# A hybrid attention layer on one core: the feed-forward part's instructions kept in the written order, a scale per token half, a pipelined output projection and spread sums

## The chip, the core and the metric

The kernel runs on one core of one Trainium2 chip. The metric is the device time of one execution in microseconds. The engines are called as in the profile: PE (TensorE, matrix products; PEld is its load of weights), DVE (VectorE), ACT (ScalarE), POOL (GpSimd) and SP (SyncE, whose queue issues the transfers). Each engine takes its instructions strictly in the order of its queue.

## What is computed

One layer over 2048 tokens of 1024 features: modulated RMS norm, an input projection, forgetting attention and differential attention, an output projection, and a modulated SwiGLU feed-forward part with 2816 hidden features. The change touches the last two steps, and a norm in the first.

```python
h = _modulate(x, ln1_g[l], sh1, sc1)
u = h @ w_in[l]
...
mixed = jnp.concatenate([fox_out, diff_out], axis=-1)
x = x + g1[:, None, :] * (mixed @ w_out[l])

h2 = _modulate(x, ln2_g[l], sh2, sc2)
y = (jax.nn.silu(h2 @ w_gate[l]) * (h2 @ w_up[l])) @ w_down[l]
x = x + g2[:, None, :] * y
```

## The kernel before

**Numbers in two halves.** PE multiplies 16-bit numbers. A 32-bit operand is scaled by a power of two and split into a high and a low half: `cast_scaled` (L139, on ACT) writes the high half, `sub_scaled` (L144, on DVE) the difference. Three products of halves make one product. The power of two comes from the operand's largest magnitude: `absmax` (L123) takes it per partition on DVE, `colmax` (L108, L109) spreads it over the partitions by a small PE matmul against an identity and reduces the result, `pow2` (L115 to L119) makes scale and inverse. So each scale is a chain DVE, PE, DVE, and PE stands at L108 until DVE has the maximum.

**Stages.** 0 to 150 us: first norm and modulation, with `first_norm` for each of the 16 blocks of 128 tokens. 150 to 1350: eight head groups of projection and attention, as streams merged by `run`. Then `out_proj` (L934) for the 16 blocks: it loads a tile of `mixed`, splits it, turns it round with a transposing transfer (L928, issued by SP), runs two halves of 24 matmuls, adds the result to x (L936), stores it as `x1d`, and takes the row's root mean square (L940 on ACT, `rsqrt`). Blocks 0 to 9 run merged with the last attention group, blocks 10 to 15 afterwards.

**Feed-forward.** 22 pairs `q`: 11 pairs of weight tiles for each of two halves of the tokens. A pair has 14 slots. Slot by slot, for `w` = gate and then up, one of seven `product`s (L1091, 12 matmuls of 512 columns each, a seven-product scheme over 2x2 blocks, in the order of `ORDER`). Its results leave PSUM through `s4s` (L1094), `s5s` (L1096), `dif` (L1101) on ACT and sums on DVE and POOL (L1097 is POOL's s4s - s5s). Beside them stand the 16 `down`s of the pair before (L1149, six matmuls each, added to x by L1153), spread over the slots by `DOWNAT`. What prepares operands is put into a slot by `at`:

- gate and up weights: `gu_load`, `gu_bound` (the maximum, 128x2048), `gu_sum` (L1038, five sums on POOL), `gu_scale` (with L108), `gu_split` in three parts (1024, 1536, 1024 wide);
- down weights: `dn_load` (transfer, maximum L1061, product L1062 on POOL), `dn_scale` (with L108), `dn_split`;
- the activation of the pair before: `act_scale` (maximum of the whole 128x2048 tile, L108) and `act_split` for each token half.

The normalised rows' sums for the seven products (`norm_row` L974 and L975, `norm_sum` L984 to L989) are made for blocks 0 to 7 next to the projection, and for blocks 8 to 15 in pairs 2, 4, 6 and 8: two rows are loaded again, normalised, and seven sums follow at slots 10 to 13. They go to `hcd` in memory and come back when the token halves change (pair 10).

**What sets the order.** The kernel is written for Tile, whose scheduler simulates the engines and places instructions as it expects them to become ready; the written order gives the dependences and the priorities. So in the kernel before neither a slot nor a stream fixes where an instruction stands on its engine. `bufs` is the number of buffers behind a name: a small tile can be written again only when its readers are done.

Of the kernel before, what the change touches and what calls it, by code (L numbers as in the profile page):

```python
# [55 lines left out]
def trunk(ctx, tc, t):
# [860 lines left out]
    def out_proj(blk):  # L917
        if blk == 0:
            hs.extend(htile() for _ in range(4))
        x1 = pairbuf(blk // 2)[:, blk % 2, :]  # L920
        rows = slice(blk * P, (blk + 1) * P)
        nc.sync.dma_start(x1, t["x"][rows, :])
# [382 lines left out]
```

## Time and profile before

| | us |
|---|---|
| median of three runs | 2928.06 |
| lowest, highest | 2925.38, 2935.83 |
| the profiled execution | 2939.51 |
| its span | 2937.7 |
| PE busy in it | 2728.9 (93%) |
| DVE busy | 2111.3 (72%) |
| POOL busy | 1609.5 (55%) |
| ACT busy | 1441.2 (49%) |
| mean granted clock of PE | 0.98 |

The profiled execution is 11.45 us above the median; all times of rows are its own, in microseconds from the start of its span. A PE group that runs without a gap shows the time of its matmuls one behind the other; idle time ahead of a group stands in brackets with what ended it. A wait is listed under the line that waited and the line that released it. The clock is the share of full speed that PE was granted; 1.00 is 2.4 GHz and 0.5 is 1.2 GHz. Shares over the whole span mix stages with different limits, so the stretches are read one by one.

### The profile page before, as it was taken

What the parts mean: (1) busy time and instruction counts of PE and PEld (TensorE: products, weight loads), DVE (VectorE), ACT (ScalarE), POOL (GpSimd) and SP (SyncE); (2) the same over time, 40 slices, a digit from 0 to 9 for tenths busy, and PEclk for the clock granted to TensorE, in tenths of its full rate; (3) what the DMA queues carried; (4) which work ended last, traced back from release to release, by engine and by line L of the source; (5) the groups of instructions that cost most, each with busy time, mean ns of one, the idle gap of its engine ahead of it and who ended that gap; (6) DMA issues with size and microseconds to landing.
All of it is one profiled execution on the core that took longest, in us unless ns stands there. A gap on an engine that the chain in (4) does not pass through costs nothing.

```text
span 2937.7 us, 49384 instructions
## 1 busy us (share of the span) xinstructions
PE 2728.9 (93%) x18902; PEld 1479.9 (50%) x18902; DVE 2111.3 (72%) x4077; ACT 1441.2 (49%) x2725; POOL 1609.5 (55%) x1392
## 2 busy tenths in 40 slices
PE   5789989899999999999989998899999999999998
PEld 3456656566665655664444343444444444444443
DVE  7786675857758686656744887787878778778775
ACT  4666667666676777786543422333323332233230
POOL 2566666665667787675542645444545444535430
PEclk9899999999999999999999999999999999999999
DMA  6232231322224233234776223224234511112101
GB/s 230 77 82 61 63 73 39 82 53 67 73 50 94 53 105 95 49 103 118 171 196 202 85 68 98 72 79 110 70 108 150 165 59 57 58 52 64 58 22 58
DMA packets 269902, 261.92 MB, mean 89 GB/s; under 512 B 204376, under 2 KB 221144, under 8 KB 263904
## 3 DMA queue, kind: packets, MB, share of 16 engines
q1 hardware_dynamic: 269664, 258.75, 31.0%
q8 instruction: 148, 2.42, 0.4%
q14 instruction: 90, 0.74, 0.1%
HBM read 173.55 MB, written 36.91 MB: 72 GB/s over the span
## 4 chain that ended last, share of the span: by engine, by line
PE 52%; DVE 21%; DMA 12%; POOL 6%; ACT 6%; issue 4%; SPq 0%; POOLq 0%; DVEq 0%; ACTq 0%
PE ps_mx L1149 10%; PE ps_ip L437 10%; PE ps_st L1091 7%; PE ps_pv L1091 6%; DMA stg<-in_w_ada_dram 3%; PE ps_ip L934 3%; DMA stg<-stg 2%; PE ps_mx L1091 2%; PE ps_st L579 2%; DVE t_mxc L548 2%; PE ps_st L580 2%; PE ps_pv L609 2%; PE ps_mx L546 2%; PE ps_pv L608 2%; PE ps_pv L607 2%
## 5 line engine op out<-in xcount | busy, mean ns | idle before, releaser
L593 POOL TENSOR_TENSOR pxs<-pxs 128x512 f16<-128x512 f32 (+3 forms) x640 | 683.3, 1082 | 325.8 <-ACT pxs L590 191.8
L1091 PEld LDWEIGHTS <-mt 128*128 128x128 f16 x3696 | 361.8, 99 | 446.7 <-issue 22.0
L437 PE MATMUL ps_ip<-wbuf,ht 128*128 128x384 f16 (+1 forms) x2952 | 560.6, 332 | 26.1 <-DVE vts L144 13.5
L1149 PE MATMUL ps_mx<-wide,ht 128*128 128x512 f16 x2112 | 505.4, 382 | 11.5 <-ACT ht L139 5.6
L1038 POOL TENSOR_TENSOR pxm<-vts 128x512 f32<-128x512 f32 x220 | 295.7, 1370 | 347.1 <-DMA vts<-in_w_gu_dram 316.3
L585 ACT ACTIVATE pxs<-ps_st,cells 128x512 f32<-128x512 f32 (+3 forms) x640 | 388.7, 619 | 142.5 <-PE ps_st L580 68.9
L437 PEld LDWEIGHTS <-ht 128*128 128x128 f16 x3072 | 295.7, 99 | 243.5 <-issue 46.2
L1091 PE MATMUL ps_st<-ht,mt 128*128 128x512 f16 x1584 | 383.0, 386 | 5.6 <-ACT mt L1094 3.2
L1091 PE MATMUL ps_pv<-ht,mt 128*128 128x512 f16 x1584 | 383.3, 380 | 1.1 <-ACT mt L1096 1.1
L590 ACT ACTIVATE pxs<-pxs 128x512 f16<-128x512 f32 (+3 forms) x640 | 350.7, 565 | 16.4 <-PE ps_pv L609 7.6
L607 PE MATMUL ps_pv<-vts,pxs 128*128 128x129 f16 (+1 forms) x2176 | 342.6, 207 | 4.2 <-DVE os L626 3.1
L608 PE MATMUL ps_pv<-vts,pxs 128*128 128x128 f16 (+1 forms) x2176 | 344.7, 208 | 0.0
L1149 PEld LDWEIGHTS <-ht 128*128 128x128 f16 x2112 | 206.3, 98 | 266.7 <-issue 16.9
L609 PE MATMUL ps_pv<-vts,pxs 128*128 128x129 f16 (+1 forms) x2176 | 325.6, 207 | 9.8 <-POOL pxs L593 8.9
L548 DVE TENSOR_REDUCE t_mxc<-ps_mx 128x1 f32<-128x512 f32 x384 | 256.9, 682 | 93.8 <-PE ps_mx L546 92.0
L1153 DVE SCALAR_TENSOR_TENSOR mt<-ps_mx,t_ai,mt 128x512 f32<-128x512 f32 x352 | 256.6, 743 | 75.5 <-PE ps_mx L1149 75.2
L607 PEld LDWEIGHTS <-pxs 128*128 128x128 f16 x2176 | 208.2, 97 | 56.7 <-ACT pxs L585 3.5
L579 PE MATMUL ps_st<-mt 67*128 67x512 f16 (+7 forms) x640 | 223.8, 350 | 10.4 <-ACT pxs L585 10.2
L609 PEld LDWEIGHTS <-pxs 128*128 128x128 f16 x2176 | 206.8, 99 | 50.0 <-POOL pxs L593 24.3
L608 PEld LDWEIGHTS <-pxs 128*128 128x128 f16 x2176 | 208.0, 97 | 35.3 <-issue 4.1
L580 PE MATMUL ps_st<-mt 128*128 128x512 f16 (+3 forms) x640 | 223.8, 350 | 0.0
L546 PE MATMUL ps_mx<-mt 71*128 71x512 f16 (+7 forms) x640 | 197.3, 350 | 19.6 <-DVE t_mxc L548 13.1
(266 smaller groups left out, 4097.0 us busy)
## 6 DMA issues: line engine op xcount, KB each, us to landing
vts<-in_w_gu_dram SPq DMA_DIRECT2D x44, 1024.0 KB
stg<-in_w_down_dram SPq DMA_DIRECT2D x44, 512.0 KB
stg<-in_w_ada_dram SPq DMA_DIRECT2D x32, 512.0 KB
stg<-in_w_in_dram SPq DMA_DIRECT2D x24, 512.0 KB
mt<-in_w_ada_dram SPq DMA_DIRECT2D x16, 512.0 KB
mt<-mt SPq DMA_DIRECT2D x128, 64.0 KB
mixed<-os SPq DMA_DIRECT2D x32, 256.0 KB
stg<-in_w_out_dram SPq DMA_DIRECT2D x16, 512.0 KB
```

The source lines that it names most:

```text
L437: T.matmul(pt[:, 0:N], lhsT=h4[:, k, hs, c : c + P], rhs=w4[k // 4][:, k % 4, ws, 0:N], start=(i == 0), stop=(i == len(terms) - 1))
L548: V.tensor_reduce(out=mx[:, 4 * j + n : 4 * j + n + 1], in_=b[:, 0:w], op=ALU.max, axis=AX.X)
L579: T.matmul(b[:, c0:QC], lhsT=K2[0:K, kb * P : (kb + 1) * P], rhs=QA[0:K, q0:q1], start=True, stop=False, skip_group_check=True)
L585: A.activation(p32[:, c0:QC], b[:, c0:QC], AF.Exp, bias=pshift, scale=1.0)
L590: A.activation(ph[:, c0:QC], p32[:, c0:QC], AF.Copy, bias=0.0, scale=1.0)
L593: (V if hilo[1] == "V" else G).tensor_tensor(out=pl[:, c0:QC], in0=p32[:, c0:QC], in1=ph[:, c0:QC], op=ALU.subtract)
L607: T.matmul(pv[:, jj, :], lhsT=lhs_h, rhs=v4[:, kb, h, 0 : W + 1], start=first, stop=False, skip_group_check=True)
L608: T.matmul(pv[:, jj, 0:W], lhsT=lhs_h, rhs=v4[:, kb, h, W + 2 : 2 * W + 2], start=False, stop=False, skip_group_check=True)
L609: T.matmul(pv[:, jj, :], lhsT=lhs_l, rhs=v4[:, kb, h, 0 : W + 1], start=False, stop=end, skip_group_check=True)
L1038: G.tensor_tensor(out=sums[:, k * 512 : (k + 1) * 512], in0=raw[:, a * 512 : (a + 1) * 512], in1=raw[:, b * 512 : (b + 1) * 512], op=op)
L1091: T.matmul(b.rearrange("p (b n) -> p b n", b=4), lhsT=aw[w][:, APOS[i] * 4 + k, ws, :], rhs=cb[:, :, 2 * k + hb, :], start=(fresh and k == ...
L1149: T.matmul(b, lhsT=aT[:, th, as_, f, j * P : (j + 1) * P], rhs=dnb[:, (2 * q + f) % 4, ws, n * 512 : (n + 1) * 512], start=(f == 0 and z = ...
```

## The change

- `Ordered` wraps an engine: each instruction issued through it is kept in program order. From the feed-forward part on (and for the functions called after that line, `out_proj` 10 to 15 among them) V, A, G and T, that is DVE, ACT, POOL and PE, are wrapped. SP isn't.
- The activation's scale is taken per token half: `act_bound` reduces 128x1024, `act_scale` makes scale and inverse, `act_split` follows. The first half's stand in slots 11, 12, 13 of the pair itself, the second half's in slots 0, 1, 2 of the next.
- `ORDER` and `DOWNAT` change; `dn_load` moves to slots 1 and 2 and its maximum becomes `dn_bound` at 3 and 4; `dn_split` moves from slots 9 and 10 to 6 and 7. The sum `tmp + dif` moves to product 3.
- Blocks 8 to 15 of the normalised rows: `late_row` inside the output projection writes them to `yd`; `late_sum` cuts each of the 28 sums into load, add (two slots on), low half (three), transpose (four) and store (five), three sums per pair, beginning at slots 6, 9 and 13. In a slot the late steps stand ahead of the others.
- `out_load` and `out_split` of the next block stand inside the current one, the split between its two halves.
- The head of the feed-forward part is put between the blocks 10 to 15.
- First norm: `first_stats` makes the row scales of four blocks together for token chunks 1 to 3. The small maxima have four buffers instead of two.

```diff
+class Ordered:
...
+        def issue(*args, **kw):
+            ins = f(*args, **kw)
+            if hasattr(ins, "ins"):
+                self.tc.keep_in_program_order(ins)
+            return ins
...
-        am = small(1, "am" if dt == F32 else "amh", bufs=2, dt=dt)
-        V.tensor_reduce(out=am, in_=src, op=ALU.max, axis=AX.X, apply_absolute_value=True)
+        am = small(1, "am" if dt == F32 else "amh", bufs=4, dt=dt)
+        V.tensor_reduce(out=am, in_=src, op=ALU.max, axis=axis, apply_absolute_value=True)
...
-            rows.append((1, lambda j=j: first_norm(j)))
+            rows.append((0.5, lambda j=j: first_scale(j, r4)))
...
+        if blk + 1 < NB:
+            out_load(blk + 1)
...
+            if n == 0 and blk + 1 < NB:
+                out_split(blk + 1)
...
+        if blk > 8:
+            late_row(blk - 1)
...
-    ORDER = (4, 5, 1, 2, 3, 7, 6)
+    ORDER = (4, 5, 1, 2, 7, 3, 6)
...
+    def late_row(blk):
+
+        y = pairbuf(blk // 2)[:, blk % 2, :]
+        norm_rows2(y, blk)
+        nc.sync.dma_start(yd[blk - 8], y)
...
+        def add():
+            e = st["e"]
+            if other:
+                G.tensor_tensor(out=e[:, 0:512], in0=e[:, 0:512], in1=e[:, 512:1024], op=op)
+            s3, hi, _, _ = parts()
+            A.activation(hi, s3, AF.Copy, bias=0.0, scale=1.0)
...
+        return [(0, load), (2, add), (3, low), (4, turn), (5, store)]
...
+    V, A, G, T = Ordered(tc, V), Ordered(tc, A), Ordered(tc, G), Ordered(tc, T)
...
+    def act_bound(q, th):
+        sets[q]["aam", th] = absmax(act[:, th], BF16, axis=AX.XY)
...
     gu_load(0, 0)
+    run(outs[10:11])
     gu_bound(0, 0)
     for k in range(5):
         gu_sum(k)
+    run(outs[11:13])
     gu_scale(0, 0)
+    run(outs[13:14])
     for k in range(3):
         gu_split(0, 0, k)
-    run(outs[10:16])
+    run(outs[14:16])
+    late_row(15)
...
-    DOWNAT = (0, 0, 0, 0, 2, 2, 2, 2, 2, 2, 1, 1, 1, 1)
+    DOWNAT = (0, 1, 1, 1, 1, 1, 2, 1, 1, 2, 2, 2, 1, 0)
...
+    for k, steps in enumerate([late_sum(jj, i) for jj in range(4, 8) for i in ORDER]):
+        for d, f in steps:
+            late[14 * (k // 3) + (6, 9, 13)[k % 3] + d].append(f)
...
-                at(3 + f, dn_load, q, f)
+                at(1 + f, dn_load, q, f)
+                at(3 + f, dn_bound, q, f)
             at(5, dn_scale, q)
             for f in range(2):
-                at(9 + f, dn_split, q, f)
+                at(6 + f, dn_split, q, f)
+        if q < NQP:
+            at(11, act_bound, q, 0)
+            at(12, act_scale, q, 0)
+            at(13, act_split, q, 0)
         if q:
-            at(0, act_scale, q - 1)
-            at(1, act_split, q - 1, 0)
+            at(0, act_bound, q - 1, 1)
+            at(1, act_scale, q - 1, 1)
             at(2, act_split, q - 1, 1)
...
-                for _ in range(DOWNAT[slot]):
+                for _ in range(DOWNAT[slot] if q < NQP else (3, 2, 2, 1, 8)[slot] if slot < 5 else 0):
...
-            for f in st[slot]:
+            for f in late[14 * q + slot] + st[slot]:
```

In the instruction streams of the changed kernel every wrapped instruction has the line L65, that of the wrapper. Three places show what moves.

DVE at the end of the output projection (`ht<-ps_ip` and `ht<-ps_mx` add a projection's half to x, `t_rq` and `cells` are the row scale, `t_amh<-vts` is `gu_bound`), before:

```order
L134 TENSOR_TENSOR t_rq_22005<-t_rq_22005,t_nv 128x1
L135 SCALAR_TENSOR_TENSOR cells<-t_rq_22005,t_ry_22003 128x1
L936 SCALAR_TENSOR_TENSOR ht<-ps_ip,cells,ht 128x512
L936 SCALAR_TENSOR_TENSOR ht<-ps_mx,cells,ht 128x512
L942 TENSOR_SCALAR t_nv<-t_nss 128x1
L1099 TENSOR_TENSOR pxm<-ps_st,mt 128x512
L133 SCALAR_TENSOR_TENSOR t_rq_22076<-t_ry_22074 128x1
L109 TENSOR_REDUCE t_cm<-ps_ip 128x1
L134 TENSOR_TENSOR t_rq_22076<-t_rq_22076,t_nv 128x1
L115 TENSOR_SCALAR t_p2a<-t_cm 128x1
L135 SCALAR_TENSOR_TENSOR cells<-t_rq_22076,t_ry_22074 128x1
```

and after:

```order
L65 SCALAR_TENSOR_TENSOR ht<-ps_ip,cells,ht 128x512
L65 SCALAR_TENSOR_TENSOR ht<-ps_mx,cells,ht 128x512
L65 TENSOR_SCALAR t_nv<-t_nss 128x1
L65 SCALAR_TENSOR_TENSOR t_rq_21984<-t_ry_21982 128x1
L65 TENSOR_TENSOR t_rq_21984<-t_rq_21984,t_nv 128x1
L65 SCALAR_TENSOR_TENSOR cells<-t_rq_21984,t_ry_21982 128x1
L65 SCALAR_TENSOR_TENSOR ht<-ht,cells,vts 128x1024
L65 TENSOR_TENSOR ht<-ht,vts 128x1024
L65 SCALAR_TENSOR_TENSOR ht<-ht,cells,vts 128x1024
L65 TENSOR_TENSOR ht<-ht,vts 128x1024
L65 TENSOR_REDUCE cells<-grep_21994 128x1
L65 TENSOR_REDUCE t_amh<-vts 128x1
```

Before, the products' sums (`pxm<-ps_st`) come in between, and the maximum of the second weight tile stands further ahead. After, the row scale of the last block, the late rows of blocks 14 and 15 (four passes over 128x1024) and the maximum of `grep2` stand ahead of `t_amh<-vts`.

DVE in slots 3 to 5 of a middle pair (`mt<-ps_mx,t_ai` is a down's L1153, `t_dam<-stg` the maximum of a down weight, `t_amh<-vts` `gu_bound`, `t_cm<-ps_ip` the step behind L108, `t_amh<-t_dam` the maximum for `dn_scale`), before, from the activation's maximum on:

```order
L1153 SCALAR_TENSOR_TENSOR mt<-ps_mx,t_ai,mt 128x512 x4
L1120 TENSOR_TENSOR pxm<-ps_mx,pxm 128x512
L144 SCALAR_TENSOR_TENSOR mt<-pxm,t_ws,mt 128x8x128
L1153 SCALAR_TENSOR_TENSOR mt<-ps_mx,t_ai,mt 128x512
L123 TENSOR_REDUCE t_amh<-uhm 128x1
L123 TENSOR_REDUCE t_amh<-vts 128x1
L1099 TENSOR_TENSOR pxm<-ps_st,mt 128x512
L109 TENSOR_REDUCE t_cm<-ps_ip 128x1
L123 TENSOR_REDUCE t_amh<-t_dam 128x1
L115 TENSOR_SCALAR t_p2a<-t_cm 128x1
```

and after:

```order
L65 SCALAR_TENSOR_TENSOR mt<-ps_mx,t_ai,mt 128x512
L65 TENSOR_REDUCE t_dam<-stg 128x1
L65 TENSOR_REDUCE t_amh<-vts 128x1
L65 TENSOR_TENSOR mt<-ps_pv,pxm 128x512
L65 SCALAR_TENSOR_TENSOR mt<-ps_mx,t_ai,mt 128x512
L65 TENSOR_REDUCE t_dam<-stg 128x1
L65 TENSOR_REDUCE t_cm<-ps_ip 128x1
```

for slots 3 and 4, and for slot 5, from the last step of `gu_scale` on:

```order
L65 TENSOR_SCALAR t_gi<-t_gi,cells 128x1
L65 TENSOR_TENSOR wide<-ps_pv,wide 128x512
L65 SCALAR_TENSOR_TENSOR mt<-ps_mx,t_ai,mt 128x512
L65 TENSOR_REDUCE t_amh<-t_dam 128x1
L65 TENSOR_REDUCE t_cm<-ps_ip 128x1
```

Before, one maximum of the activation and one of the weight follow each other, and the one for `dn_scale` stands behind several other steps. After, the maxima stand directly behind a down's evacuation, the last of them (`t_amh<-t_dam`) with nothing else in between.

ACT at the start of a pair with a late sum (`mt<-ps_st` is `s4s`, `mt<-ps_pv` `s5s`, `mt<-vts,t_ws` and `mt<-pxm,t_ws` the three casts of `gu_split`, `stg<-stg` the cast of a normalised rows' sum, `ht<-uhm` the activation's cast), before:

```order
L1094 ACTIVATE mt<-ps_st 128x512
L988 ACTIVATE stg<-stg 128x4x128
L1096 ACTIVATE mt<-ps_pv 128x512
L139 ACTIVATE mt<-pxm,t_ws 128x8x128
L988 ACTIVATE stg<-stg 128x4x128
L1101 ACTIVATE wide<-ps_st 128x512
L988 ACTIVATE stg<-stg 128x4x128
L1094 ACTIVATE mt<-ps_st 128x512
L139 ACTIVATE ht<-uhm,t_as 128x1024 x2
L139 ACTIVATE mt<-vts,t_ws 128x8x128
L139 ACTIVATE mt<-pxm,t_ws 128x12x128
L1103 ACTIVATE uhm<-ps_st,t_gi 128x512
```

and after:

```order
L65 ACTIVATE mt<-ps_st 128x512
L65 ACTIVATE mt<-vts,t_ws 128x8x128
L65 ACTIVATE mt<-ps_pv 128x512
L65 ACTIVATE stg<-stg 128x4x128
L65 ACTIVATE mt<-pxm,t_ws 128x12x128
L65 ACTIVATE mt<-pxm,t_ws 128x8x128
L65 ACTIVATE ht<-uhm,t_as 128x1024
L65 ACTIVATE wide<-ps_st 128x512
```

Before, the sums' casts come four near one another, between the evacuations. After, there is one in this stretch, directly behind `s5s` and ahead of the second and third cast of the weight.

## Rows read from the trace of the kernel before

**Rows 1.** Busy time by stretch: columns us, then busy us of each engine, clock, DMA share, GB/s

```profile
1532.00:1603.00 71.00, 62.79 (x285) 27.92 (x283) 31.06 (x49) 16.18 (x28) 20.38 (x13) 0.95 0.69 214
...
1603.00:2342.00 739.00, 688.71 (x3135) 306.65 (x3132) 578.78 (x827) 236.37 (x279) 375.93 (x241) 0.97 0.33 102
...
2342.00:2900.00 558.00, 557.94 (x2606) 253.54 (x2607) 426.70 (x634) 169.78 (x191) 236.56 (x161) 1.00 0.15 50
```

**Rows 2.** PE's waits, 1603 to 2938: waiting line, releaser, us in all, times, longest

```profile
PE ps_ip L108 <- DVE t_amh L123: 36.9, 8, 7.3
```

**Rows 3.** PE's waits, 150 to 1603

```profile
PE ps_ip L934 <- DMA wide<-wide: 5.7, 3, 2.3
```

**Rows 4.** Timeline of PE, five stretches: start, us, line, count, [idle before <-releaser]

```profile
1413.41 7.04 PE L934 MATMUL ps_ip<-mt,wide 128*128 128x512 f16 x24 [2.27 <-DMA wide<-wide]
...
1569.24 5.78 PE L934 MATMUL ps_mx<-mt,wide 128*128 128x512 f16 x26
...
1975.83 1.47 PE L1149 MATMUL ps_mx<-wide,ht 128*128 128x512 f16 x6 [1.14 <-ACT ht L139]
...
2211.52 4.44 PE L1149 MATMUL ps_mx<-wide,ht 128*128 128x512 f16 x12 [2.06 <-DVE mt L1153]
...
2902.64 1.46 PE L1149 MATMUL ps_mx<-wide,ht 128*128 128x512 f16 x6
...
2908.59 0.29 PE L108 MATMUL ps_ip<-idb,t_amh 128*128 128x128 bf16 x1 [4.50 <-DVE t_amh L123]
...
2910.88 23.08 PE L1149 MATMUL ps_mx<-wide,ht 128*128 128x512 f16 x96 [2.00 <-ACT ht L139]
```

**Rows 5.** Timeline of DVE at the end, 2902 to 2910

```profile
2902.84 0.69 DVE L1120 TENSOR_TENSOR pxm<-ps_mx,pxm 128x512 f32<-128x512 f32 x1 [1.84 <-PE ps_mx L1091]
...
2904.14 0.75 DVE L1153 SCALAR_TENSOR_TENSOR mt<-ps_mx,t_ai,mt 128x512 f32<-128x512 f32 x1 [0.61 <-PE ps_mx L1149]
...
2906.25 2.29 DVE L123 TENSOR_REDUCE t_amh<-uhm 128x1 bf16<-128x2048 f32 x1 [1.36 <-POOL uhm L1126]
...
2908.92 0.29 DVE L109 TENSOR_REDUCE t_cm<-ps_ip 128x1 f32<-128x128 f32 x1 [0.39 <-PE ps_ip L108]
...
2909.43 0.15 DVE L116 TENSOR_SCALAR t_as<-t_p2a 128x1 int32<-128x1 int32 x1
...
2909.51 0.14 DVE L118 TENSOR_SCALAR t_p2b<-t_p2a 128x1 f32<-128x1 f32 x1
...
2909.87 0.27 DVE L1136 TENSOR_SCALAR t_ai<-t_ai,t_di,t_gi 128x1 f32<-128x1 f32 x1
```

**Rows 6.** DVE by shape, 1603 to 2938: shapes xcount, busy us, mean ns, idle before

```profile
L144 DVE SCALAR_TENSOR_TENSOR mt<-pxm,t_ws,mt 128x1536 f16<-128x1536 f32 x43 | 81.6, 1897 | 1.8 <-ACT mt L139 1.8
...
L144 DVE SCALAR_TENSOR_TENSOR mt<-pxm,t_ws,mt 128x1024 f16<-128x1024 f32 x43 | 72.5, 1687 | 6.3 <-ACT mt L139 5.6 <-POOL mt L1097 0.7
...
L144 DVE SCALAR_TENSOR_TENSOR mt<-vts,t_ws,mt 128x1024 f16<-128x1024 f32 x43 | 59.4, 1381 | 5.1 <-ACT mt L139 4.2
...
L144 DVE SCALAR_TENSOR_TENSOR ht<-uhm,t_as,ht 128x1024 f16<-128x1024 f32 x44 | 55.7, 1296 | 9.3 <-ACT ht L139 9.2
...
L1061 DVE TENSOR_REDUCE t_dam<-stg 128x1 f32<-128x1024 f32 x41 | 49.3, 1210 | 13.4 <-DMA stg<-in_w_down_dram 12.9
```

**Rows 7.** ACT by shape, 1603 to 2938

```profile
L139 ACT ACTIVATE mt<-pxm,t_ws 128x1536 f16<-128x1536 f32 x43 | 67.2, 1563 | 26.4 <-DVE t_ws L116 26.4
...
L139 ACT ACTIVATE mt<-vts,t_ws 128x1024 f16<-128x1024 f32 x43 | 49.0, 1141 | 106.7 <-PE ps_mx L1149 59.1 <-DVE t_p2b L118 35.5 <-DVE t_gi L119 10.4
...
L1094 ACT ACTIVATE mt<-ps_st 128x512 f32<-128x512 f32 x43 | 25.3, 589 | 66.1 <-PE ps_st L1091 66.1
```

**Rows 8.** POOL by shape, 1603 to 2938

```profile
L1097 POOL TENSOR_TENSOR mt<-mt 128x512 f32<-128x512 f32 x44 | 62.7, 1424 | 60.3 <-ACT mt L1096 60.3
...
L984 POOL TENSOR_TENSOR stg<-stg 128x512 f32<-128x512 f32 x20 | 29.5, 1473 | 103.3 <-DMA hcd<-stg 101.0 <-DVE wide L144 2.4
```

**Rows 9.** Timeline of SP's queue, one transpose

```profile
1409.65 1.33 SPq L928 DMA_TRANSPOSE wide<-wide  x1
```

More of the change, by code (lines that the diff above doesn't have):

```diff
@@ L292, in first_norm, with first_stats, first_scale @@
         norm_rows(xt, xt)
+    def first_stats(c, r4):
+        ss = small(4, "dss", bufs=2)
+        for j in range(4):
+            A.activation(sqs.bitcast(F16), xcs[c][:, j, :], AF.Square, bias=0.0, scale=1.0, accum_out=ss[:, j : j + 1])
+        V.tensor_scalar(out=ss, in0=ss, scalar1=1.0 / D, scalar2=EPS, op0=ALU.mult, op1=ALU.add)
+        r = small(4, "drr", bufs=2)
+        rsqrt(ss, r, 4)
+        r4["r"] = r
+    def first_scale(blk, r4):
+        xt = xcs[blk // 4][:, blk % 4, :]
+        G.tensor_scalar(out=xt, in0=xt, scalar1=r4["r"][:, blk % 4 : blk % 4 + 1], scalar2=0.0, op0=ALU.mult, op1=ALU.add)
     def first_hT(blk):
@@ L915, in pairbuf, with out_load, out_split @@
         return t.rearrange("p (b n) -> p b n", b=2)
[L917 to L922, printed above, removed]
+    oin = {}
+    def out_load(blk):
         mt = stage()
-        nc.sync.dma_start(mt, mixed[rows, :])
+        nc.sync.dma_start(mt, mixed[blk * P : (blk + 1) * P, :])
+        oin[blk] = mt
+    def out_split(blk):
+        mt = oin.pop(blk)
         mh, mT = scr[:, 0], scr[:, 1 + blk % 2].rearrange("p s (k n) -> p s k n", k=KT)
@@ L928, in out_proj @@
         nc.sync.dma_start(mT.rearrange("p s k n -> p (s k) n"), mh.rearrange("p s n -> p (s n)"), transpose=True)
+    def out_proj(blk):
+        if blk == 0:
+            hs.extend(htile() for _ in range(4))
+            out_load(0)
+            out_split(0)
+        mT = scr[:, 1 + blk % 2].rearrange("p s (k n) -> p s k n", k=KT)
+        x1 = pairbuf(blk // 2)[:, blk % 2, :]
+        rows = slice(blk * P, (blk + 1) * P)
+        nc.sync.dma_start(x1, t["x"][rows, :])
+        if blk + 1 < NB:
+            out_load(blk + 1)
         for n in range(2):
@@ L1107, in product @@
             V.tensor_tensor(out=dif, in0=b, in1=dif, op=ALU.subtract)
+            G.tensor_tensor(out=tmp, in0=tmp, in1=dif, op=ALU.add)
             if w == 0:
@@ L1112, in product @@
         elif i == 7:
+            V.tensor_tensor(out=s5s, in0=b, in1=tmp, op=ALU.add)
             if w == 0:
-                V.tensor_tensor(out=act[:, 0, 0], in0=b, in1=tmp, op=ALU.add)
-                A.activation(act[:, 0, 0], act[:, 0, 0], AF.Silu, bias=0.0, scale=gi)
+                A.activation(act[:, 0, 0], s5s, AF.Silu, bias=0.0, scale=gi)
             else:
-                V.tensor_tensor(out=s5s, in0=b, in1=tmp, op=ALU.add)
                 G.tensor_tensor(out=act[:, 0, 0], in0=s5s, in1=act[:, 0, 0], op=ALU.mult)
@@ L1152, in down @@
         xs = xb[:, n * 512 : (n + 1) * 512]
-        V.scalar_tensor_tensor(out=xs, in0=b, scalar=sets[q]["ai"], in1=xs, op0=ALU.mult, op1=ALU.add)
+        V.scalar_tensor_tensor(out=xs, in0=b, scalar=sets[q]["ai", th], in1=xs, op0=ALU.mult, op1=ALU.add)
         if q % NPAIR == NPAIR - 1:
@@ L1191, in trunk @@
         f(*a)
+    late = [[] for _ in range(14 * (NQP + 1))]
+    for k, steps in enumerate([late_sum(jj, i) for jj in range(4, 8) for i in ORDER]):
+        for d, f in steps:
+            late[14 * (k // 3) + (6, 9, 13)[k % 3] + d].append(f)
     for q in range(NQP + 1):
```

83 lines of the change are left out of this document (45 added, 38 removed).

## The prediction

> **What bounds the kernel now.** I first cut the span into stages with the table of busy time by stretch [rows 1] and looked for the stretches in which TensorE (PE) is not busy throughout. From 2342 on it is full (557.94 of 558 us, clock 1.00): there the feed-forward part runs at the rate of its matmuls. From 1603 to 2342 it has 688.71 of 739 us at clock 0.97, and around the end of the output projection 62.79 of 71. So the room is in the first half of the feed-forward part and just ahead of it. Then I read the waits [rows 2]: eight waits at L108, 36.9 us, for the row maximum of a weight tile or of the activation (L123). L108 is a matmul by which PE spreads that maximum over the partitions; PE takes its instructions in order, so everything behind it stands still. The projection waits three times for a transposed tile, 5.7 us [rows 3]. Last, single groups of matmuls give the price of a gap [rows 4]: 26 matmuls in a row take 5.78 us and 6 take 1.47, so one more costs 0.216. Those 6 stand behind a gap of 1.14 and still run at full speed. After a gap of 2.06 the next 12 take 4.44 instead of 2.75: 1.69 more, at the lower of the two clock levels.
>
> The floor: a pair has 168 product matmuls and 96 of the downs, 264 x 0.216 = 57.0, with its four L108s (0.06 of PE each) 57.2. Twenty-two make 1258. The profiled stretch from 1603 to the last matmul's end (2910.88 + 23.08 = 2934) is 1331, and about 40 matmuls (8 us) of it ran before 1603: 1339. **The part loses 81 us today**, 8.7 of them at its very end (gaps of 4.50 and 2.00, and 96 matmuls at 23.08 where full speed gives 20.9) [rows 4].
>
> **The change, part by part.** The pinning takes away the scheduler's order, and with it every long wait that came of it. What it puts there must be summed: PE now meets each L108 right behind the slot's last down, and DVE and ACT must have got there through everything written ahead. Terms: a matmul's issue end to the evacuation's start 0.20 (the next group starts at 2902.64, DVE at 2902.84); DVE's end to L108 0.05 (2906.25 + 2.29, 2908.59); an evacuation 0.69, a down's 0.75 [rows 4, 5]. A slot with one down is 18 matmuls, 3.89 us of PE.
> (a) Slot 1, second half's act_scale: from the end of slot 0's product 0.20, ACT's s4s 0.59, its cast 1.14, DVE's difference 1.38, act_bound, 0.05 [rows 6, 7]. act_bound over 128x1024 is new; bounds 0.69 (a 512-wide pass) and 2.29 (the 2048-wide one), taken 1.21, the reduction of the same width. Sum 4.57 against 3.89: **0.68**.
> (b) Slot 4, gu_scale of the next pair: from the end of slot 3, 0.20 + 0.75 + dn_bound 1.21 + gu_bound 2.29 + 0.05 = 4.50 against 3.89: **0.61**.
> (c) Slot 5, dn_scale: nothing for PE lies between the slot's down and L108: 0.20 + 0.75 + a one-column reduction (0.15, as the small steps of rows 5) + 0.05 = **1.15**.
> Together 2.44 a pair in 21 pairs: **51**. No other L108 of a pair has less than 5 us of matmuls between its bound and itself, and I cost these at nothing; if that cover fails, it is about 1 us a pair, 22 in all. Each of (a) to (c) is below the 1.14 after which the clock held, or at it.
>
> The **late sums** are three a pair. The third has its load at slot 13, so its add falls in slot 1 of the next pair, ahead of everything else of that slot. POOL first makes s4s - s5s (1.42), then the add (1.47); ACT's cast of the sum waits for that, and behind it on ACT wait the casts of gu_split, behind them DVE's differences, and behind those dn_bound and gu_bound, for which PE waits in (b). From the end of slot 1's product: 0.20 + 0.59 + 1.42 + 1.47 + 0.59 (the cast, sized like s4s) + 1.56 + 1.90 + the scale's six small steps 1.22 (2908.92 to 2910.14) + 0.69 + 0.75 + 0.75 (the low half, as a 512-wide pass) + 1.69 + 1.30 + 0.75 + 1.21 + 2.29 + 0.05 = 18.4 [rows 5 to 8]. PE has the down, wait (a) and three slots: 1.30 + 0.68 + 11.67 = 13.65. So (b) becomes 4.8 instead of 0.61, 4.2 more, and such a gap costs the clock 1.69 besides: 5.9. Of the nine pairs with a sum there, seven have the add (two of the seven kinds of sum have one operand): 7 x 5.9 = 41. The two others spare the 2.89 of POOL and pay 1.3 each: 3. **44**, bounds 0 (the add is there before ACT comes to it) and 60 (each of the nine as dear, with a second slow stretch). The bursts that these sums replace are part of the 81 that go.
>
> Smaller: pair 0 has to fill its queues, 5 (0 to 8); the reload of seven 1 MB pieces between the token halves is unchanged in size, 3 (0 to 7); the end, with the second half's split ahead of the last downs, 5 (4 to 9) where it was 8.7; the extra scale chain, 1.2 of DVE a pair, lies beside matmuls. The part becomes 1258 + 51 + 44 + 5 + 3 + 5 = 1366 against 1339: **+27**.
>
> **Output projection.** Blocks 0 to 9 get their tile loaded and split a block ahead; the three waits for a transpose, 5.7 in all, go [rows 3]: **-5** (0 to -6, since the scheduler still places them). Blocks 10 to 15 are pinned. A block is two halves of 24 matmuls, 5.18 each; the next block's split now stands on DVE behind the first half's evacuation, and its transposed tile has the second half to arrive: 0.20 + 0.75 + 1.38 (a difference 1024 wide) + 3.76 (a transpose issued at 1409.65 lets PE go at 1413.41) [rows 4 to 6, 9] = 6.1 against 5.18: 0.9 a block. The small steps of the row scale and the late row (two 1024-wide passes, 1.30 + 1.21) reach the next first half's end about even. So 5 over five blocks (0 to 10). What is written between the blocks comes on top, since DVE has no slack there: gu_bound 2.29, a scale chain 1.22 and three differences 4.97 of weight (0,0): 8.5 (bounds 0 and 8.5). Behind the last block PE has nothing until up_head's second L108: 0.20 + 0.75, the square 1.14 (as ACT's 1024-wide cast) and nine small steps with their hand-overs, 3.0 [rows 5, 7], two late rows 5.0, grep2's maximum 1.2, gu_bound 2.29, 0.05: 12.5. Two long gaps at 1.7 of clock: 3.4. Sum 29 against 11 today (8.2 idle, and at clock 0.95 about 3 more) [rows 1]: **+18**. The batched row statistics of the first stage turn twelve small chains to three on engines that are not the bound there: 0, plus or minus 5.
>
> The sum: 27 - 5 + 18 = **+40**. The profiled execution (2939.51) lies 11.4 above the median; I add the differences to the median: 2928 + 40 = 2968.
>
> **One rule weighed.** The gap of 1.14 left the matmuls behind it at full speed [rows 4]; waits (a) to (c) are of that size but come back in every pair. The Trainium skill, "TensorE: Matmul & The Clock Gate", section "A second HAM failure mode: psum-queue depth-cycling", says that a PE that idles briefly between groups of matmuls, often enough, makes the clock swing between its levels. By the row the waits cost their length alone; by the rule every pair pays for a slow stretch too. The row is single gaps, so it doesn't settle what recurring ones do; this is rival 3.
>
> **Rivals.** 1, faster: the late sums and the pinned tail cost nothing extra, since DVE's and ACT's queued instructions overlap where I add full lengths. In the scale chain steps of 0.15 start 0.08 apart (2909.43, 2909.51), which speaks for it; between dependent wide passes no row shows it. Its place is the queue between slot 1's product and slot 4's L108, and it decides where that queue falls from 18.4 to 13.65; the tail follows with the same overlap. Then 2968 - 44 - 22 = 2902 (of the tail only 7 stays of 29, less than today).
> 2, the same: only the late sums are free (the add done before ACT needs it; against it stands that POOL can't start it before s5s of the same slot). 2968 - 44 = 2924.
> 3, slower still: wait (c), 1.15 just behind (b), lets the clock fall in every pair: 21 x 1.69 = 35 more, 3003. For it: gaps of 2.06 did it, and (b) and (c) lie 4 us apart. Against: the 1.14.
> That the order isn't kept as written is excluded by the instruction streams: from block 10 on they stand as written on PE, DVE, ACT and POOL.
>
> **How the numbers follow.** Forecast 2968 (own range 2945 to 2995): 0.46. Rival 1: 0.18, rival 2: 0.19, rival 3: 0.17. A measurement of this kernel tells about 0.5% (15 us) from no change. Rival 2's spread of 15 puts 0.04 of it into faster: faster 0.22, same 0.15, slower 0.63. The range reaches to both outer rivals, 2893 to 3006.
>
> **What would show it.** Right: eight long waits at L108 gone, instead some 60 short ones in slots 1, 4 and 5, the latter near 1.15; in pairs 1 to 9 gaps near 5 at slot 4 with a slow stretch behind, none in pairs 11 to 20; a DVE that is full from 1540 to 1610 and a gap of about 12 before the first product. Wrong: PE full in pairs 1 to 9 (rivals 1, 2), or a clock under 0.97 in pairs 11 to 20 (rival 3). The forecast also falls if a queue that I took as covered, POOL's gu_sums or SP's loads, turns out to end last.

## The result

| | before | after |
|---|---|---|
| median, us | 2929.69 (4 runs, 2925.38 to 2935.83) | 2978.94 (4 runs, 2972.82 to 2981.84) |
| profiled execution, us | 2939.51 | 2972.82 |
| its span, us | 2937.7 | 2971.0 |

The change makes the kernel slower: ratio 1.0165, 95% interval 1.0144 to 1.0187, 49 us by the medians. The two profiled executions lie 33 us apart, since that of before is slower than the four runs of its row and that of after is the quickest of its own; a sum of stages out of the two traces can only account for those 33.

The stretches of the kernel after: busy time of PE, PEld, DVE, ACT, POOL, then clock, DMA share and GB/s.

```profile
1530.00:1622.00 92.00, 61.92 (x255) 25.97 (x253) 44.70 (x65) 17.25 (x31) 12.21 (x9) 0.85 0.72 220
1622.00:1700.00 78.00, 63.18 (x277) 27.24 (x277) 54.23 (x87) 27.77 (x33) 36.78 (x25) 0.93 0.28 88
1700.00:2200.00 500.00, 470.47 (x2162) 209.50 (x2163) 381.28 (x616) 155.58 (x184) 233.90 (x165) 0.99 0.32 98
2200.00:2900.00 700.00, 683.29 (x3183) 306.18 (x3182) 529.57 (x856) 211.83 (x239) 297.16 (x211) 1.00 0.23 76
```

Against [rows 1]: the tail of the projection, 62.79 of 71 us before, is now a stretch of 92 us with 61.92 busy at clock 0.85. The later feed-forward part, full before, idles 17 of 700 us. Its waits (line of PE, releaser, us in all, times, longest), from 1500 on:

```profile
PE ps_ip L65 <- DVE t_amh L65: 74.3, 66, 13.0
PE ps_ip L65 <- DMA wide<-wide: 11.9, 4, 5.5
PE ps_ip L65 <- DVE t_cm L65: 5.9, 1, 5.9
```

Eight long waits at L108 [rows 2] have become 66, and all but a few are short: three in a pair, as expected. PE's timeline of two stretches, the tail (1521 to 1623) and an ordinary pair's slots 1 to 5, shows where:

```profile
1521.56 6.20 PE L65 MATMUL ps_ip<-mt,wide 128*128 128x512 f16 x24
...
1537.03 6.98 PE L65 MATMUL ps_ip<-mt,wide 128*128 128x512 f16 x24 [4.09 <-DMA wide<-wide]
...
1566.80 7.44 PE L65 MATMUL ps_ip<-mt,wide 128*128 128x512 f16 x24 [5.86 <-DVE t_cm L65]
...
1596.61 7.90 PE L65 MATMUL ps_ip<-mt,wide 128*128 128x512 f16 x24 [5.46 <-DMA wide<-wide]
...
1622.64 0.29 PE L65 MATMUL ps_ip<-idb,t_amh 128*128 128x128 bf16 x1 [12.95 <-DVE t_amh L65]
1622.74 4.21 PE L65 MATMUL ps_st<-ht,mt 128*128 128x512 f16 x12
...
2299.55 0.23 PE L65 MATMUL ps_ip<-idb,t_amh 128*128 128x128 bf16 x1 [0.29 <-DVE t_amh L65]
...
2311.71 0.23 PE L65 MATMUL ps_ip<-idb,t_amh 128*128 128x128 bf16 x1 [0.28 <-DVE t_amh L65]
...
2316.74 0.23 PE L65 MATMUL ps_ip<-idb,t_amh 128*128 128x128 bf16 x1 [0.91 <-DVE t_amh L65]
```

The three rows from 2299 on are waits (a), (b) and (c). The idle time in brackets is counted from the modelled end of the last matmul, 0.16 after the next one could have been issued, so they cost about 0.45, 0.45 and 1.07. A pair takes 59.27 (the next wait (c) is at 2376.01) where its matmuls take 57.2.

A late sum with an add costs what the next rows show; first two such pairs on PE, then the chain of the first on POOL, ACT and DVE:

```profile
1757.36 0.23 PE L65 MATMUL ps_ip<-idb,t_amh 128*128 128x128 bf16 x1 [3.13 <-DVE t_amh L65]
1757.43 2.75 PE L65 MATMUL ps_pv<-ht,mt 128*128 128x512 f16 x12
...
1878.88 0.29 PE L65 MATMUL ps_ip<-idb,t_amh 128*128 128x128 bf16 x1 [3.13 <-DVE t_amh L65]
1878.96 4.11 PE L65 MATMUL ps_pv<-ht,mt 128*128 128x512 f16 x12
```

```profile
1741.47 1.27 POOL L65 TENSOR_TENSOR mt<-mt 128x512 f32<-128x512 f32 x1 [2.78 <-ACT mt L65]
1742.69 1.26 POOL L65 TENSOR_TENSOR stg<-stg 128x512 f32<-128x512 f32 x1
```

```profile
1743.99 0.63 ACT L65 ACTIVATE stg<-stg 128x512 f16<-128x512 f32 x1 [2.60 <-POOL stg L65]
1744.53 2.60 ACT L65 ACTIVATE mt<-pxm,t_ws 128x1536 f16<-128x1536 f32 x2
```

```profile
1746.12 1.82 DVE L65 SCALAR_TENSOR_TENSOR mt<-pxm,t_ws,mt 128x1536 f16<-128x1536 f32 x1 [3.18 <-ACT mt L65]
...
1755.03 2.27 DVE L65 TENSOR_REDUCE t_amh<-vts 128x1 bf16<-128x2048 f32 x1
```

ACT stands 2.60 us for POOL's add, DVE 3.18 for ACT's cast behind it, and PE 3.13 for the maximum at the end of DVE's queue. Seven pairs have such a gap (at 1695, 1757, 1879, 1942, 2066, 2129, 2191), the two with a one-operand sum only 0.42 (1817, 2003), none later ones. That is the list of the prediction.

### The profile page after: what moved, and what is told of

The parts are those of the page before. It is cut to its first block, busy times and chain, and to the rows that moved or that the text cites. A ratio compares the mean times of both kernels' runs of the same rounds, so it can differ in the third digit from the quotient of the medians.

```text
span 2971.0 us, 49657 instructions
## 1 busy us (share of the span) xinstructions
PE 2733.1 (92%) x18924; PEld 1477.9 (50%) x18924; DVE 2111.4 (71%) x4195; ACT 1434.0 (48%) x2704; POOL 1568.0 (53%) x1392
## 5 line engine op out<-in xcount | busy, mean ns | idle before, releaser
L65 PEld LDWEIGHTS <-mt 128*128 128x128 f16 x3696 | 359.7, 99 | 422.5 <-issue 12.3
L65 PE MATMUL ps_mx<-wide,ht 128*128 128x512 f16 x2112 | 497.6, 379 | 1.8 <-DVE ht L65 1.7
L617 ACT ACTIVATE pxs<-ps_st,cells 128x512 f32<-128x512 f32 (+3 forms) x640 | 388.2, 619 | 128.1 <-PE ps_st L612 58.3
L65 POOL TENSOR_TENSOR pxm<-vts 128x512 f32<-128x512 f32 x220 | 287.4, 1324 | 180.6 <-DMA vts<-in_w_gu_dram 148.6
L65 PE MATMUL ps_pv<-ht,mt 128*128 128x512 f16 x1584 | 371.9, 386 | 0.0
L65 PE MATMUL ps_st<-ht,mt 128*128 128x512 f16 x1584 | 364.6, 380 | 0.0
L65 DVE SCALAR_TENSOR_TENSOR mt<-ps_mx,t_ai,mt 128x512 f32<-128x512 f32 x352 | 261.7, 747 | 115.7 <-PE ps_mx L65 113.3
L65 PEld LDWEIGHTS <-ht 128*128 128x128 f16 x2112 | 206.5, 98 | 251.9 <-DVE ht L65 2.7
L65 POOL TENSOR_TENSOR stg<-stg,grep 128x1024 f32<-128x1024 f32 x44 | 103.5, 2352 | 220.0 <-DVE t_dam L65 163.6
```

Source lines behind the costliest of these rows:

```text
L65: ins = f(*args, **kw)
L617: A.activation(p32[:, c0:QC], b[:, c0:QC], AF.Exp, bias=pshift, scale=1.0)
```

## The experiments

The theory after the result: the loss is a sum of separate pieces (late sums, short waits, pipelined projection, pinned tail), each at the place that the prediction named. The general rival: the scheduler lays everything out anew, and pieces can't be told apart.

**1. The first stage alone** (`first_only`), into the kernel before:

```diff
+        rows = [(0, lambda: hts.append(htile())), (2, lambda: first_stats(c, r4))]
...
-            rows.append((1, lambda j=j: first_norm(j)))
+            rows.append((0.5, lambda j=j: first_scale(j, r4)))
```

> The kernel before with the batched row statistics of the first stage alone. In the changed kernel the attention part runs 12 to 17 us earlier than before from 290 us on. Theory: the batching is the cause, so this kernel is 10 to 14 us faster than before (about 2917) and its attention runs 12 us earlier. Rival: the lead comes from elsewhere in the change (four buffers of the small maxima, another layout by the scheduler); then this kernel is within 4 us of before. My prediction had 0, plus or minus 5, for this term.

Measured 2930.7 beside 2930.7, ratio 1.000 (0.999 to 1.001): nothing. The theory falls here and the prediction's 0 stands; the lead of 12 us had been read off two single executions, of which that of before lies 10 us above its kernel's median. One pair of profiled executions doesn't carry a term of 10 us.

**2. The pipelined projection alone** (`pipe_only`), into the kernel before, nothing pinned:

```diff
+            out_load(blk + 1)
...
+            if n == 0 and blk + 1 < NB:
+                out_split(blk + 1)
```

> The kernel before with the pipelined output projection alone (load and split of the next block inside the current one), nothing pinned. In the changed kernel the 12 us of lead are gone by the end of block 9. Theory: the pipelined split costs them, since it sits in the queues of DVE, ACT and SP that the last attention group uses; this kernel is 5 to 12 us slower than before. Rival (my prediction): the waits for a transpose go and it is 0 to 6 us faster; then the loss belongs to the late rows or to the pinning of what follows.

Measured 2938.0 beside 2930.7, ratio 1.0028 (1.0011 to 1.0045): some 8 us slower, 3 to 13 by the interval. My -5 had the wrong sign (it was for blocks 0 to 9, this kernel has all 16). The waits for a transpose between 1350 and 1521 do go, 5.7 to 0, but others take their place. PE's waits for DVE's evacuation of a projection's half there, before:

```profile
PE ps_ip L934 <- DVE ht L936: 2.9, 4, 1.7
PE ps_ip L934 <- DVE uhm L936: 2.9, 4, 0.9
```

and here, with the attention's wait for POOL, which was 0.6 before:

```profile
PE ps_ip L948 <- DVE uhm L950: 6.2, 4, 3.2
PE ps_ip L948 <- DVE ht L950: 4.6, 2, 2.5
PE ps_pv L609 <- POOL pxs L593: 4.3, 4, 1.6
```

That points to DVE's and POOL's queues. It is read from one execution of each, and no run took the split out of a single queue.

**3. Pinning only behind block 15** (`pin_after_out`):

```diff
-    V, A, G, T = Ordered(tc, V), Ordered(tc, A), Ordered(tc, G), Ordered(tc, T)
     NPAIR = NFF // 2
...
     late_row(15)
+    V, A, G, T = Ordered(tc, V), Ordered(tc, A), Ordered(tc, G), Ordered(tc, T)
```

> The changed kernel, but the engines are wrapped only behind block 15 and the last late row, so blocks 10 to 15 and the first weight's preparation between them are placed by the scheduler. Theory: the written order of the tail costs about 28 us against before (five waits of 1.2 to 5.9 between blocks with a slow clock behind them, and 13 ahead of the first product); this kernel gains 15 to 28 us on the changed one, about 2955. Rival: the tail is long by its dependences (transposes, late rows), not by the order; then it gains less than 5.

Measured 2971.8, ratio 1.0141 (1.0125 to 1.0158) beside 1.0165: 7 us, near the rival. The many waits become two long ones, PE's timeline:

```profile
1552.35 1.03 PE L982 MATMUL ps_ip<-mt,wide 128*128 128x512 f16 x2 [10.74 <-DMA wide<-wide]
...
1611.53 0.29 PE L65 MATMUL ps_ip<-idb,t_amh 128*128 128x128 bf16 x1 [14.79 <-DVE t_amh L65]
```

So the written order of the tail is worth about 7 us. Whether the rest of its loss comes with the transposed tile inside half a block or with the late rows, this run doesn't separate; experiment 11 does in part.

**4. Late steps last in their slot** (`late_last`):

```diff
-            for f in late[14 * q + slot] + st[slot]:
+            for f in st[slot] + late[14 * q + slot]:
```

> The changed kernel with the late steps of a slot behind the slot's other steps instead of ahead of them. Theory: in seven pairs PE waits 3.3 us at slot 4 because the late sum's cast holds ACT behind POOL's add, ahead of the weight's casts; with the casts ahead of it those seven gaps go to about 0.3 and the clock loss with them: 20 to 28 us faster than the changed kernel, about 2955. Rival: the engines' total work in slots 1 to 4 is what lasts, whatever its order; then less than 8 us.

Measured 2951.9, ratio 1.0080 (1.0065 to 1.0096): 27 us faster than the changed kernel (medians), the upper end of the theory. All the work is still done; only its place in the queues differs. Waits of PE behind 1700, first of the changed kernel, then of this one:

```profile
PE ps_ip L65 <- DVE t_amh L65: 46.9, 59, 3.1
```

```profile
PE ps_ip L65 <- DVE t_amh L65: 31.5, 58, 0.9
```

The waits of 3.1 are gone; the clock of 1700 to 2200 is back at 1.00.

**5. dn_scale a slot later** (`dn_late`), on the changed kernel:

```diff
-            at(5, dn_scale, q)
+            at(5, dn_max, q)
+            at(6, dn_scale, q)
             for f in range(2):
-                at(6 + f, dn_split, q, f)
+                at(7 + f, dn_split, q, f)
```

> The changed kernel with dn_scale's L108 one slot later (its maximum stays in slot 5, the splits move to slots 7 and 8), so a slot of matmuls stands between the maximum and L108. Theory: wait (c) of 1.1 us in 21 pairs is idle time on the path; it goes and nothing takes its place: 20 to 25 us faster than the changed kernel, about 2956. Rival: the later waits (a) and (b) grow by what (c) gave DVE as a head start; then less than 8 us.

Measured 2954.1, ratio 1.0079 (1.0062 to 1.0096): 25 us faster, as the theory has it; the rows give 21 times 1.07, 22. Wait (c) is idle time on the path, and PE pays its full length in each pair.

**6. All three waits a slot later** (`waits_later`), with the edits of experiments 4 and 5:

```diff
...
-            at(1, act_scale, q - 1, 1)
-            at(2, act_split, q - 1, 1)
+            at(2, act_scale, q - 1, 1)
+            at(3, act_split, q - 1, 1)
...
-            at(4, gu_scale, q + 1, 0)
+            at(5, gu_scale, q + 1, 0)
```

> The changed kernel with the late steps last in their slot and all three of the short waits given a slot of matmuls: act_scale of the second half at slot 2 (split at 3), gu_scale at slot 5, dn_scale at slot 6 (splits at 7 and 8). Theory: a pair falls from 59.3 us to its matmuls' 57.2: 21 times 2.07 = 43 us faster than the kernel with the late steps last (2952), about 2909, faster than before. Rival: DVE's queue is then the limit and the waits reappear at other slots; then less than 20 us.

Measured 2910.5, ratio 0.9930 (0.9906 to 0.9953): 41 us below the 2951.9 of experiment 4, of 43 expected, and faster than before. Its stretch from 1700 to 2800 has no idle PE left:

```profile
1700.00:2800.00 1100.00, 1100.00 (x5170) 501.53 (x5168) 885.58 (x1428) 353.45 (x408) 541.02 (x368) 1.00 0.28 92
```

DVE, busy 886 of 1100 us, was no limit; where its results were asked for was.

**7. Wait (c) doubled** (`gap2`): one more reduction, whose result nobody uses, ahead of dn_scale's maximum.

```diff
+        V.tensor_reduce(out=dmy, in_=e["st", 1], op=ALU.max, axis=AX.X, apply_absolute_value=True)
         g = colmax(absmax(e["dam"], BF16), "ip")
```

> The changed kernel with one more reduction of 128x1024 (1.21 us, its result unused) on DVE ahead of dn_scale's maximum, so wait (c) is about 2.3 us in every pair instead of 1.1. Theory: the wait costs its length, 21 to 22 times 1.2 = 26 us, and at 2.3 us, a size after which a single gap lost 1.69, the clock falls in every pair as well: 26 + 36 = 62 us, and the granted clock from 2400 to 2900 falls to about 0.97. Rival: only the length, 26 us, clock 1.00 there.

One run, 3012.4, 33 above the changed kernel, between the two. PE's timeline of two neighbouring pairs:

```profile
2456.30 0.23 PE L65 MATMUL ps_ip<-idb,t_amh 128*128 128x128 bf16 x1 [2.21 <-DVE t_amh L65]
2456.37 2.75 PE L65 MATMUL ps_mx<-ht,mt 128*128 128x512 f16 x12
...
2516.87 0.29 PE L65 MATMUL ps_ip<-idb,t_amh 128*128 128x128 bf16 x1 [2.21 <-DVE t_amh L65]
2516.95 4.40 PE L65 MATMUL ps_mx<-ht,mt 128*128 128x512 f16 x12
```

The same gap of 2.21 is followed once by 12 matmuls in 2.75, full speed, and once by 12 in 4.40. The ten pairs from 2271 to 2885 take 60.57 (five) or some 62.2 (five): 1.3 more than 59.27 by length, and in every second pair on average 1.7 more by the clock. So the clock isn't lost in each, which is why 62 was too much.

**8. Less ahead of the first product** (`tail_free`), with the late steps last: the second weight's gu_scale in slot 3 of pair 0, late rows 14 and 15 in its slots 4 and 6, the next pair's load two slots later there.

```diff
-    for _, f, *a in up_head(0):
+    for _, f, *a in up_head(0)[:-1]:
...
+                at(3, gu_scale, 0, 1)
+                at(4, late_row, 14)
+                at(6, late_row, 15)
```

> The changed kernel with the late steps last in their slot, and of the tail the late rows 14 and 15 and the second weight's gu_scale moved into slots 3 to 6 of the first pair (the next weight's load and scale two slots later there). Theory: the 13 us ahead of the first product are DVE's queue (two late rows, two maxima) ahead of one L108, none of which the first products need: 12 to 15 us faster than the kernel with the late steps last (2952), about 2938. Rival: the first products wait for something else (their split weight or rows); then less than 4 us.

Measured 2947.1, ratio 1.0054 (1.0037 to 1.0071): 5 us beside experiment 4. The 12.95 ahead of the first product is gone, and there is a new gap in slot 5 of pair 0:

```profile
1645.11 0.29 PE L65 MATMUL ps_ip<-idb,t_amh 128*128 128x128 bf16 x1 [10.69 <-DVE t_amh L65]
```

The L108 there is `dn_scale`'s, and one of the moved late rows now stands ahead of its maximum: DVE hadn't less to do; PE met it 22 us later.

**9. No pinning** (`no_pin`): the changed kernel without the line that wraps the engines.

> The changed kernel with no engine wrapped: all slots, splits and late sums as changed, the order left to the scheduler. Theory: pinning trades long waits at L108 (36.9 us before) for short ones; without it the long waits come back (five or more of over 4 us between 1650 and 2400) while the short ones of 0.9 to 1.1 in the later pairs go: about 2965, plus or minus 15. Rival: the loss of the change lies in the written order alone, and without it the kernel is at 2935 or below, near the one before.

Measured 2941.8, ratio 1.0041 (1.0026 to 1.0056): the written order as it stands costs 37 of the 49 us, and the rest of the change some 12, of which the projection's 8 is one. Between theory and rival, and below the theory's range. The stretch 1700 to 2200, and PE's largest group of waits from 1540 on:

```profile
1700.00:2200.00 500.00, 453.21 (x2050) 199.45 (x2048) 376.01 (x586) 148.94 (x177) 242.41 (x153) 0.98 0.30 92
```

```profile
PE ps_mx L1233 <- DVE mt L1237: 17.0, 17, 4.1
```

Unpinned, this stretch is worse than in the changed kernel (470.47), not by long waits at L108 but by many of the downs for DVE; from 2200 on it is full, 678.77 of 680. The long waits at L108 that the theory expected back stay away; from 1540 on there are, where before had 36.9 in eight [rows 2],

```profile
PE ps_ip L126 <- DVE t_amh L141: 3.2, 2, 3.0
```

So the rest of the change is enough to remove them, without the pinning; which part of it does, no run separates. With the waits out of the written order the pinned kernel of experiment 6 is 31 us faster than this one; an unpinned kernel with the same moves wasn't run.

**10. Late rows in slots 8 and 10** (`tail_rows_later`), experiments 6 and 8 together, and pair 1's second gu_scale in slot 13 of pair 0; against experiment 8:

```diff
-                at(4, late_row, 14)
-                at(6, late_row, 15)
+                at(8, late_row, 14)
+                at(10, late_row, 15)
```

> The kernel with the late steps last and the three short waits a slot later (2911), and in the tail the second weight's gu_scale in slot 3 of the first pair, the late rows 14 and 15 in its slots 8 and 10, and the next pair's second gu_scale in its slot 13. When the late rows stood in slots 4 and 6 the 13 us ahead of the first product only moved to slot 5 (10.7). Theory: DVE has some 20 us of work ahead of slot 6 of the first pair, the late rows 5 of it, and has room behind slot 7: 8 to 14 us faster, about 2900. Rival: pair 0 is bound by DVE as a whole, since no downs stretch its slots; then less than 5.

Measured 2905.0, ratio 0.9912 (0.9895 to 0.9929): 5 us beside experiment 6, just above the rival's bound and far from the theory. A gap of 13.20 stands behind 13 products of pair 0, that is in slot 12, now.

**11. The old tail** (`old_tail`): as 10, but the output projection of before, pinning only behind block 15, and the first weight prepared ahead of block 10 as before (late rows 8 to 13 stay in the projection).

```diff
...
-    run(outs[10:11])
...
-    run(outs[14:16])
+    run(outs[10:16])
+    V, A, G, T = Ordered(tc, V), Ordered(tc, A), Ordered(tc, G), Ordered(tc, T)
```

> As the kernel before this one, with the output projection as it was (a block's split at its own head), blocks 10 to 15 and the first weight unpinned and in the old order. Theory: the pipelined split costs 8 (measured alone) and the pinned tail's waits for transposes about 12 with 7 of clock; back in the scheduler's hands the tail loses 11: 15 to 22 us faster than with the new tail, about 2882. Rival: the late rows of blocks 8 to 13, which the old projection didn't have, hold it as well; then less than 6.

Measured 2891.1, ratio 0.9864 (0.9847 to 0.9880): 14 us faster than 10, near the theory's 15, and 40 us faster than the kernel before. Three edits stand in it together, so the 14 can't be shared out among them; but the late rows of blocks 8 to 13 are still there, so it wasn't these that held the 14, and the rival falls.

**12. Pair 1's second weight later still** (`pair_one`), on 11: its maximum and sums in slot 13 of pair 0, its scale and splits in slot 3 of pair 1.

```diff
-                at(3, gu_scale, 0, 1)
+            if q < 2:
+                at(3, gu_scale, q, 1)
```

> The kernel with the old tail (2891), and the second weight of pair 1 prepared later: its maximum and sums in slot 13 of pair 0 instead of 10, its scale and splits in slot 3 of pair 1, and the load of pair 2 two slots later, as pair 0 already has it. PE there waits 13.2 us at the L108 in slot 13 of pair 0. Theory: the wait is DVE's queue (late rows, maxima and splits against slots of 2.6 us without downs); pair 1 has downs and DVE catches up in it: 8 to 14 us faster, about 2880. Rival: the wait moves into pair 1 as it moved from the tail to slot 5 and from there to slot 13; then less than 4.

Measured 2890.5, ratio 0.9853 (0.9836 to 0.9870): the same as 11. The gap is still there, 3 us shorter; first 11, then 12:

```profile
1655.88 0.29 PE L65 MATMUL ps_ip<-idb,t_amh 128*128 128x128 bf16 x1 [13.20 <-DVE t_amh L65]
```

```profile
1656.88 0.29 PE L65 MATMUL ps_ip<-idb,t_amh 128*128 128x128 bf16 x1 [10.12 <-DVE t_amh L65]
```

The expectation names the wrong L108. In both kernels 13 products lie between the part's first one and the gap, so PE stands in slot 12, where `act_scale` asks for the maximum of the first half's activation. DVE's rows of kernel 11 say the same: the maximum that ends just before 1655.88 is that of `uhm`, and the scale made from it is `t_as`:

```profile
1654.60 1.22 DVE L65 TENSOR_REDUCE t_amh<-uhm 128x1 bf16<-128x1024 f32 x1 [1.38 <-POOL uhm L65]
...
1657.43 0.15 DVE L65 TENSOR_SCALAR t_as<-t_p2a 128x1 int32<-128x1 int32 x1
```

The `gu_scale` that was moved out of slot 13 had no wait of its own (in kernel 11 its L108 follows at 1660.03 without idle time). Moving its maximum took 2.28 us of DVE from ahead of the gap, and the gap fell by 3.1, but the median didn't. So this run doesn't test the theory, nor the rival. In kernel 11 DVE is busy 49.31 of the 60 us around the gap (third number with a count):

```profile
1640.00:1700.00 60.00, 45.83 (x209) 20.38 (x208) 49.31 (x74) 19.63 (x24) 32.46 (x20) 0.89 0.36 114
```

I take the head of the part to be bound by the chain of DVE and POOL there. That is argued from these rows; no run moved `act_scale` in pair 0 or took work away.

## Why the prediction was right, and where not

It gave 2968 (2893 to 3006) and slower; measured 2979. The direction holds, and so do the short waits and the late sums, place by place. That the sum came within 11 us is luck: the feed-forward part was put 21 us too high, the way up to its first product 15 too low, and 16 of the 49 us lie between the profiled executions and the medians. By its own steps:

| step | predicted | measured |
|---|---|---|
| feed-forward part in all | 1366 | 1622.7 to 2967.3: 1344.6, before 1339 |
| up to its first product, against before | +13 | +28, the rest of the 33 |
| waits (a), (b), (c), a pair | 0.68 + 0.61 + 1.15 = 2.44 | 59.27 - 57.2 = 2.07; of them (c) 1.07 |
| all three in 21 pairs | 51 | 41 (experiment 6) |
| late sums | 44 | 27 (experiment 4) |
| pair 0 | 5 | some 13 |
| change of the token half | 3 | 0 (the period there is 59.27 too) |
| the end | 5 | about 2 (gaps of 1.43 and 0.31 among the last downs) |
| blocks 0 to 9, pipelined | -5 | +8 for the whole projection (experiment 2) |
| the pinned tail, its loss | 29 | 40 (39 and 1.5 of clock, below) |
| first stage | 0 | 0 (experiment 1) |

- **What takes the long waits away.** The prediction lets the pinning do it. That step failed: the rest of the change removes them without any pinning, 3.2 us instead of 36.9 (experiment 9). The sum didn't rest on it, since it prices what the written order puts in their place.
- **Late sums.** Place, cause and list of pairs were right; the term was mis-sized. Gap 3.3 (3.13 and 0.16) instead of 4.8: DVE's passes ran at 1.82 and 1.28 where I took the means 1.90 and 1.69 of [rows 6], POOL's two at 1.27 and 1.26 instead of 1.42 and 1.47 [rows 8], and neighbours overlap a little (1743.99 + 0.63 is past 1744.53). The shorter passes make about 1.0 of the 1.5, the overlap the rest. That is rival 1's mechanism, at a third of the size that it needed. And I charged the clock's 1.69 seven times: behind three of the seven gaps (as at 1757.36) the 12 matmuls took 2.75, behind four 4.11 to 4.44 (as at 1878.96). Seven gaps, each 2.85 longer than a later pair's 0.28, and 6.4 of clock are 26, which agrees with experiment 4.
- **Pair 0.** I gave 5 for filling the queues, without a sum, and at most 8. It loses some 19 from the first product (1622.74) to wait (c) of pair 1 (1700.27): 77.5 for 270 matmuls, 58.3 at 0.216; of it pair 1's own waits are 4.8 and the slow first group 1.5. Most of the 13 that are left is one gap and the slow group behind it:

```profile
1666.01 0.29 PE L65 MATMUL ps_ip<-idb,t_amh 128*128 128x128 bf16 x1 [7.83 <-DVE t_amh L65]
1666.09 4.72 PE L65 MATMUL ps_pv<-ht,mt 128*128 128x512 f16 x12
```

 What the term left out, as far as the rows show: without downs a slot is 2.6 us of PE, while DVE's and POOL's work for the next weights is the same. That this makes the gap is argued.
- **The tail.** From block 10's first matmul (1521.56) to the first product (1622.74) 101.2 us for six blocks of 10.36: 39, and 1.5 of slow clock behind. My final gap (12.5 against 12.95 idle) was met, in part by luck: DVE's two late rows there hold a wait for the store of `x1d` that the sum didn't have, and shorter small steps made up for it:

```profile
1616.71 1.28 DVE L65 SCALAR_TENSOR_TENSOR ht<-ht,cells,vts 128x1024 f32<-128x1024 f32 x1 [1.36 <-DMA x1d<-ht]
```

 Two terms were too small. The clock: four first halves at 6.20, 6.98, 7.44 and 7.90 where 5.34 is full speed, and the first products at 4.21, 8.6 in all where I had 3.4 (the 6.20 stands behind the attention's last matmuls, not behind a gap of the tail). And the waits between the blocks, 11.9 for transposes and 5.9 for `t_cm`, where I had 5 for the transposes and 8.5 for DVE's work. The transpose was timed by a single one at 3.76 [rows 9], which took 1.33 to issue; the trace before also has one of 8.67, and in the tail after they take 1.85 to 5.12:

```profile
1547.20 8.67 SPq L928 DMA_TRANSPOSE wide<-wide  x1
```

```profile
1529.81 5.12 SPq L964 DMA_TRANSPOSE wide<-wide  x1
...
1546.06 2.00 SPq L964 DMA_TRANSPOSE wide<-wide  x1
```

 PE goes on at 1537.03, 7.2 after the first's issue, and at 1550.35, 4.3 after the second's. Why the issue takes so differently long stays open. The sign that DVE would be full from 1540 to 1610 failed: it is busy 30.71 of 70 us, so where I wrote that DVE has no slack, PE waits for chains (evacuation, split, transpose; row scale and late row ahead of `t_cm`) while DVE is idle more than half of the time:

```profile
1540.00:1610.00 70.00, 56.01 (x235) 23.78 (x233) 30.71 (x48) 12.99 (x22) 7.68 (x5) 0.90 0.67 201
```
- **Blocks 0 to 9.** The step "the three waits for a transpose go" was right as far as the wait goes (0.4 us is left of 5.7), and wrong in what it is worth: waits for DVE's evacuation and for POOL take their place, and the whole edit costs 8 (experiment 2).
- **The rule weighed.** With waits of 0.45, 0.45 and 1.07 us in every pair the clock from 2200 to 2900 is 1.00; the row was the better guide, and rival 3 falls. At 2.2 in every pair (experiment 7) half of the pairs have a slow stretch: that far the sentence of the Trainium skill, "TensorE: Matmul & The Clock Gate", section "A second HAM failure mode: psum-queue depth-cycling", on recurring short idling agrees with the trace.
- **Rival 2** (the add is there before ACT needs it) is excluded by ACT's row at 1743.99, which waits 2.60 for POOL.

What the 16 us between the medians' 49 and the profiles' 33 are in terms of stages stays open.

## What to carry to other kernels

When the order is written by hand, write each request for another engine's result one slot of the bottleneck engine's own work behind the result, and put work that nobody waits for soon (late sums) last in its slot: two edits of this kind turned 1.7% slower into 0.7% faster. Before pinning, add up, for every instruction on which the bottleneck engine stands, the queue written ahead of it on the engine that releases it; mean lengths, one behind the other, came out half as long again as the gap that was measured (4.8 for 3.3). Add up dependent chains too, since an engine that is idle half of the time can still be waited for. When a wait wanders as instructions are moved, find out first, from the releasing engine's rows, which request it now stands at: the last edit here moved another one.
